# Gate and up products of four feed-forward layers as seven half-size products in Strassen's manner, with the sums of their operands made on the chip

## Chip, core and metric

The kernel runs as one program on one core of a Trainium2 chip. The metric is the device time of one execution in microseconds (us); lower is better. The engines are TensorE (PE: products, with its weight loads as PEld), VectorE (DVE), ScalarE (ACT), GpSimd (POOL) and SyncE (SP, which issues the DMAs here).

## What is computed

The network works on 512 tokens of 1024 features. A first block of two attention layers gives x; then come two layers, each of a feed-forward step, a mixer, a cross-attention and a second feed-forward step, and a last norm. The change is in the four feed-forward steps, of which the reference says:

```python
D_FF = ((8 * D_MODEL // 3 + 127) // 128) * 128      # 2816

def rmsnorm(x, g):
    xf = x.astype(jnp.float32)
    y = xf * lax.rsqrt(jnp.mean(xf * xf, axis=-1, keepdims=True) + NORM_EPS)
    return (y * g.astype(jnp.float32)).astype(x.dtype)

def swiglu(h, w_in, w_out):
    gate, up = jnp.split(h @ w_in, 2, axis=-1)
    return (jax.nn.silu(gate) * up) @ w_out
```

A step is x + 0.5 * swiglu(rmsnorm(x, g), w_in, w_out), with w_in of 1024 x 5632 and w_out of 2816 x 1024, everything in float32.

## The kernel before

Activations have their features on partitions: x is eight tiles `xr` of [128, 512 tokens]. A float32 operand a is kept as hi + lo (hi its rounding to float32r), and a product is three passes, hi\*hi, hi\*lo and lo\*hi: `Net.mm3` (L127) issues the three matmuls of a chunk of 128 features on L131, L132 and L133. `Net.split` (L113) makes hi by a copy on ACT (L114) and lo by a subtraction on DVE (L115), whose two inputs lie in SBUF. `Net.weight` (L117) loads a weight piece of 512 KB into `ws` (three buffers, in a pool that lives through the whole program) by a DMA that SP issues (L121), and splits it into `wh`, `wl` of [128, 1024] (four buffers each).

A feed-forward step, `Block2.ffn` (L1185), begins with `norm` (L1125): for each chunk of x, hi and lo of x times the norm's gain (`nh`, `nl`, L1132 on ACT and L1133 on DVE), and its square, summed over the chunks by POOL into `acc` (L1141). The tiles `nh`, `nl` and `acc` are in the pool `norm`, which is opened once for all steps. `stats` (L1144) makes `rb`, 1/rms of each token along rows, by two small products and a chain of small DVE instructions (`Net.rsqrt`, L145 to L155).

Then 22 chunks j of 128 hidden features follow in groups of 8, 8 and 6. For each j there is a gate product `pg` and an up product `pu`, each of 8 chunks of features x 3 passes, a matmul with 512 columns (tokens) each time. After them:

```python
t = pool.tile([P, S], F32, name="g", tag="g")
nc.vector.tensor_tensor(t, pg, self.rb, op=OP.mult)
nc.scalar.activation(t, t, AF.Silu)
nc.gpsimd.tensor_tensor(out=t, in0=t, in1=self.rb, op=OP.mult)
u = pool.tile([P, S], F32, name="u", tag="u")
nc.vector.tensor_tensor(u, pu, t, op=OP.mult)
```

and u is split into `hh`, `hl`. These are lines L1197 to L1204. When a group's hidden chunks are there, eight output products add to x (L1212); in the very last group they run in two cuts of 256 tokens, so that the last norm can follow the first cut.

No order is written out by hand in a feed-forward step: a scheduler, which goes by a timeline of its own, places each engine's instructions. Each engine then runs its instructions in that order and waits for semaphores. Pools of a stage are opened and closed with it, and a later pool that gets the same memory waits until the earlier one's last reader is done.

## Time and profile before

| | us |
|---|---|
| median of 3 runs (range) | 3713.2 (3712.51 to 3716.09) |
| span of the profiled execution | 3715.2 |
| PE busy | 3618.4 (97%) |
| PE weight loads busy | 2996.4 (81%) |
| DVE busy | 2070.7 (56%) |
| ACT busy | 1375.2 (37%) |
| POOL busy | 762.7 (21%) |

The span is that of one profiled execution; it is 2.0 us above the median of the timed runs. Busy shares are averages over the whole program. Matmuls overlap in the array, so a PE that is 97% busy says that products follow each other with hardly a pause; what one product costs is the distance between the starts of two that follow each other. An instruction's recorded time on DVE or POOL includes the time it is held up after it has started.

### The profile page before, as it was taken

The page shows a single profiled execution, that of the slowest core. Times are in us where ns is not written, and L with a number is a line of the kernel's source. Part 1 is how long each engine was busy: PE and PEld are TensorE (multiplying, and loading weights), DVE is VectorE, ACT ScalarE, POOL GpSimd, SP SyncE. Part 2 cuts the span into 40 slices and gives each one's busy share as a digit, 9 for nine tenths or more (in the row PEclk, how much of TensorE's full clock was granted, in tenths as well). Part 3 has the DMA queues.
Part 4 walks back from the last instruction along what each step waited for, and adds up shares of the span by engine and source line. Part 5 has one row for each costly group of instructions (what it writes and reads, how often), then busy time and mean ns, then how long its engine had stood idle before and what let it go on. Part 6 is the DMA issues. An engine that isn't in the chain of part 4 may idle for free.

```text
span 3715.2 us, 51467 instructions
## 1 busy us (share of the span) xinstructions
PE 3618.4 (97%) x19706; PEld 2996.4 (81%) x19706; DVE 2070.7 (56%) x4209; ACT 1375.2 (37%) x2407; POOL 762.7 (21%) x908
## 2 busy tenths in 40 slices
PE   8999999999999999999999999999999999999998
PEld 6887778888887778888778888888888888788887
DVE  6665763376566464334766433443347887664335
ACT  4334443233345432223654322322233333443223
POOL 1222330032233011102320100210025444101001
PEclk9999999999999999999999999999999999999999
DMA  8434113143322333333122333333333212322333
GB/s 276 128 111 136 58 49 128 63 142 88 88 70 67 139 100 102 97 94 105 58 91 63 108 97 97 97 97 97 97 100 112 57 56 74 115 75 93 101 98 103
DMA packets 135718, 364.35 MB, mean 98 GB/s; under 512 B 30000, under 2 KB 43184, under 8 KB 134960
## 3 DMA queue, kind: packets, MB, share of 16 engines
q1 hardware_dynamic: 135472, 361.06, 31.2%
q8 instruction: 155, 2.54, 0.3%
q14 instruction: 91, 0.75, 0.1%
HBM read 331.64 MB, written 19.66 MB: 95 GB/s over the span
## 4 chain that ended last, share of the span: by engine, by line
PE 87%; DVE 6%; ACT 2%; DMA 2%; issue 1%; POOL 1%; SPq 0%; DVEq 0%; ACTq 0%; POOLq 0%
PE p L131 15%; PE p L133 15%; PE p L132 15%; PE pS L131 7%; PE pS L132 6%; PE pS L133 6%; PE po L519 2%; PE pT L132 2%; PE pT L131 2%; PE pT L133 2%; PE po L132 2%; PE po L131 2%; PE po L133 2%; DVE wl L115 1%; PE pS L493 1%
## 5 line engine op out<-in xcount | busy, mean ns | idle before, releaser
L114 ACT ACTIVATE wh<-ws 128x1024 fp32r<-128x1024 f32 (+4 forms) x561 | 563.7, 1006 | 1421.8 <-PE p L132 683.8
L115 DVE TENSOR_TENSOR wl<-ws,wh 128x1024 fp32r<-128x1024 f32 (+3 forms) x542 | 640.4, 1182 | 252.7 <-ACT wh L114 250.8
L131 PE MATMUL p<-nh,wh 128*128 128x512 f32 x1084 | 429.1, 397 | 4.5 <-ACT nh L1132 2.0
L133 PE MATMUL p<-nh,wl 128*128 128x512 f32 x1084 | 424.7, 392 | 4.7 <-DVE wl L115 4.7
L132 PE MATMUL p<-nl,wh 128*128 128x512 f32 x1084 | 424.2, 391 | 1.9 <-DVE nl L115 1.9
L1199 POOL TENSOR_TENSOR g<-g,rb 128x512 f32<-128x512 f32 x88 | 149.8, 1704 | 1137.1 <-ACT g L1198 1137.1
L131 PE MATMUL pS<-nh,wh 128*128 128x512 f32 x620 | 254.5, 411 | 1.0 <-DVE xr L1182 1.0
L133 PEld LDWEIGHTS p<-nh,wl 128*128 128x128 f32 x1084 | 203.5, 188 | 50.3 <-DVE wl L115 6.2
L133 PE MATMUL pS<-nh,wl 128*128 128x512 f32 x620 | 242.8, 392 | 0.0
L132 PE MATMUL pS<-nl,wh 128*128 128x512 f32 x620 | 242.6, 391 | 0.0
L131 PEld LDWEIGHTS p<-nh,wh 128*128 128x128 f32 x1084 | 203.6, 188 | 46.8 <-ACT nh L1132 2.5
L132 PEld LDWEIGHTS p<-nl,wh 128*128 128x128 f32 x1084 | 203.7, 188 | 42.2 <-DVE nl L115 2.2
L1197 DVE TENSOR_TENSOR g<-p,rb 128x512 f32<-128x512 f32 x88 | 60.4, 691 | 227.8 <-PE p L133 217.6
L131 PE MATMUL p<-hxh,wh 128*128 128x512 f32 (+1 forms) x456 | 183.9, 403 | 0.8 <-DVE wT L502 0.8
L132 PE MATMUL p<-hl,wh 128*128 128x512 f32 (+1 forms) x488 | 179.8, 369 | 0.0
L133 PE MATMUL p<-hh,wl 128*128 128x512 f32 (+1 forms) x488 | 179.4, 368 | 0.0
L131 PE MATMUL p<-hh,wh 128*128 128x512 f32 (+1 forms) x488 | 179.3, 368 | 0.0
L1141 POOL TENSOR_TENSOR acc<-acc,sq 128x512 f32<-128x512 f32 x48 | 73.5, 1532 | 477.4 <-ACT sq L1140 477.0
L133 PE MATMUL p<-hxh,wl 128*128 128x512 f32 (+1 forms) x456 | 170.5, 374 | 0.0
L132 PE MATMUL p<-hxl,wh 128*128 128x512 f32 (+1 forms) x456 | 170.5, 374 | 0.0
L509 POOL TENSOR_SCALAR p<-p,rinv 128x768 f32<-128x768 f32 (+2 forms) x128 | 104.3, 815 | 254.0 <-DVE rinv L508 145.7
L1212 DVE SCALAR_TENSOR_TENSOR xr<-p,xr 128x512 f32<-128x512 f32 (+1 forms) x68 | 42.5, 627 | 170.0 <-PE p L133 169.9
(592 smaller groups left out, 8864.2 us busy)
## 6 DMA issues: line engine op xcount, KB each, us to landing
ws<-in_ffn_w_in_dram SPq DMA_DIRECT2D x176, 512.0 KB
ws<-in_ffn_w_out_dram SPq DMA_DIRECT2D x64, 512.0 KB
ws<-in_w_in_tok_dram SPq DMA_DIRECT2D x52, 512.0 KB
wh<-in_w_ada_dram SPq DMA_DIRECT2D x48, 512.0 KB
ws<-in_ffn_w_out_dram SPq DMA_DIRECT2D x40, 384.0 KB
ws<-in_w_out_dram SPq DMA_DIRECT2D x24, 512.0 KB
ws<-in_dn_qkv_dram SPq DMA_DIRECT2D x24, 512.0 KB
ws<-in_xa_wk_dram SPq DMA_DIRECT2D x16, 512.0 KB
```

The costliest lines, as they stand in the source:

```text
L114: self.last_hi = self.nc.scalar.activation(hi, src, AF.Copy)
L115: (eng or self.nc.vector).tensor_tensor(out=lo, in0=src, in1=hi.bitcast(F32), op=OP.subtract)
L131: mm(pt, sh, mh, start=first and i == 0, stop=False)
L132: mm(pt, sh, ml, start=False, stop=False)
L133: mm(pt, sl, mh, start=False, stop=last and i == n - 1)
L493: mm(ps, q, kA[:, k0:k1], start=True, stop=False)
L509: nc.gpsimd.tensor_scalar(p, p, r, 0.5, op0=OP.mult, op1=OP.mult)
L519: self.net.nc.tensor.matmul(ps[h:h + HD, :], v, w, start=i < 2, stop=i >= len(parts) - 2)
L1141: (nc.vector if c == 7 else nc.gpsimd).tensor_tensor(out=acc, in0=acc, in1=sq, op=OP.add)
L1197: nc.vector.tensor_tensor(t, pg, self.rb, op=OP.mult)
L1199: nc.gpsimd.tensor_tensor(out=t, in0=t, in1=self.rb, op=OP.mult)
L1212: nc.vector.scalar_tensor_tensor(x, ps, 0.5, x, op0=OP.mult, op1=OP.add)
```

## The change

The two products of a chunk j, gate and up, are taken as one product of [512 tokens x 1024] with [1024 x 256], each side cut in half: tokens and features of x into X11, X12, X21, X22, and the weight into B11, B21 (gate) and B12, B22 (up). `USES` names the seven products: P1 to P7, each over 512 features (4 chunks x 3 passes, matmuls with 256 columns), with operands that are blocks or sums of blocks. Outside the feed-forward steps the program's source is the same (comments and descriptions are gone, so lines after the first move by a few).

`halves` takes the place of `norm` in these steps: it scales each chunk of x into `xg`, forms S1 to S4 of the tokens' side, and splits the seven tokens' operands into hi and lo; `xg`, `xh` and the temporaries are in pools that are opened in the step. `sums` loads the weights of a chunk j into `wg`, `wu` (four buffers, in the step's own pool) and forms T3 and T1 on DVE, T2 and T4 on POOL. `operands` splits seven weight operands of [128, 512]. `gated` adds the products up: some are accumulated in a PSUM bank, with copies of the bank between (`s1`, `sV`, `sU`, on ACT), and the gate, in two halves of 256 tokens, goes through DVE, POOL, ACT and POOL again. PE's order is written out by hand in the loop over j; P3 and P4 of a chunk come after P1, P7 and P6 of the next. The other engines' order is still the scheduler's.

```diff
+    USES = dict(P1=("X11", "B11"), P2=("X12", "B21"), P3=("S4", "B22"), P4=("X22", "T4"), P5=("S1", "T1"),
+                P6=("S2", "T2"), P7=("S3", "T3"))
...
+        for c in range(8):
+            if c % 2 == 0:
+                xg.append(hold.tile([P, 2 * S], F32, name="xg", tag="hd", bufs=8))
+            v = xg[-1].rearrange("p (h c t) -> p h c t", h=2, c=2)[:, :, c % 2, :]
+            nc.scalar.activation(v, self.x[c].rearrange("p (h t) -> p h t", h=2), AF.Copy, scale=g[:, c:c + 1])
+            p = c // 2 % 2
+            if c % 2:
+                a11, a21 = xg[p][:, :S], xg[p][:, S:]
+                if c < 4:
+                    put("X11", p, a11)
+                    s3 = tmp("s3", "t")
+                    nc.vector.tensor_tensor(s3, a11, a21, op=OP.subtract)
+                    put("S3", p, s3)
+                else:
...
+    def sums(self, wg, wu, pool):
...
+        G, U = (pool.tile([P, 1024], F32, name=n, tag="wr", bufs=4) for n in ("wg", "wu"))
+        nc.sync.dma_start(G, wg)
+        nc.sync.dma_start(U, wu)
+        B = dict(B11=G[:, :512], B21=G[:, 512:], B12=U[:, :512], B22=U[:, 512:])
+        for n, a, b, eng in (("T3", "B12", "B22", nc.vector), ("T1", "B11", "B12", nc.vector),
+                             ("T2", "T1", "B22", nc.gpsimd), ("T4", "T2", "B21", nc.gpsimd)):
+            B[n] = pool.tile([P, 512], F32, name=n, tag=n, bufs=2)
+            eng.tensor_tensor(out=B[n], in0=B[a], in1=B[b], op=OP.add)
+        return B
...
+        def gate(sl, snap, bank):
+            v, rb = t[:, sl], self.rb[:, sl]
+            nc.vector.tensor_tensor(v, ps[bank], st[snap], op=OP.add)
+            nc.gpsimd.tensor_tensor(out=v, in0=v, in1=rb, op=OP.mult)
+            nc.scalar.activation(v, v, AF.Silu)
+            nc.gpsimd.tensor_tensor(out=v, in0=v, in1=rb, op=OP.mult)
...
-                for j in range(k0, k0 + kn):
-                    pg = self.fm(win[l, j], self.h)
-                    pu = self.fm(win[l, 22 + j], self.h)
...
+                        mm(j, made, "P1")
+                        mm(j, made, "P7")
+                        if more:
+                            operands(j + 1, "B11", "T3")
+                        if cur:
+                            mm(j - 1, cur, "P3")
+                        mm(j, made, "P6")
+                        if cur:
+                            mm(j - 1, cur, "P4")
+                        operands(j, "B22", "T4")
...
+                        mm(j, made, "P2")
+                        if more:
+                            operands(j + 1, "T2", "B21")
+                        if j:
+                            mm(j, made, "P5")
+                        if more:
+                            operands(j + 1, "T1")
```

The output products of a group (`ffn_out`) take the first two chunks of x without the group's last hidden chunk, and add that after; they are the same products as before.

How the order of the instructions moves is shown at two places. The first is DVE in the loop over j, in the middle of a group. Before, one chunk j (L115 is lo of a split):

```order
L1197 TENSOR_TENSOR g<-p_15105,rb 128x512
L115 TENSOR_TENSOR wl<-ws,wh 128x1024
L1201 TENSOR_TENSOR u<-pS,g 128x512
L115 TENSOR_TENSOR wl<-ws,wh 128x1024
L115 TENSOR_TENSOR hl<-u,hh 128x512
```

In the changed kernel, the first twelve of the fifteen rows of a chunk (L116 is lo of a split; `hd` is the hidden chunk; `pS`, `po` and `p3` are PSUM banks):

```order
L1263 TENSOR_TENSOR T3_15090<-wu_15087 128x512
L1263 TENSOR_TENSOR T1_15092<-wg_15086,wu_15087 128x512
L1308 TENSOR_TENSOR u1_15080<-pS_14955,sU_15078 128x256
L116 TENSOR_TENSOR hd_14815<-u_14814,hd_14815 128x512
L116 TENSOR_TENSOR wl_15131<-wg_15086,wh_15130 128x512
L116 TENSOR_TENSOR wl_15131<-T3_15090,wh_15130 128x512
L1315 TENSOR_TENSOR u_14958<-p3_14954,t_14957 128x256
L1299 TENSOR_TENSOR t_14957<-pS_14955,sV_15017 128x256
L116 TENSOR_TENSOR wl_15183<-wu_14943,wh_15182 128x512
L116 TENSOR_TENSOR wl_15183<-T4_14952,wh_15182 128x512
L1299 TENSOR_TENSOR t_15101<-po_15100,s1_15116 128x256
L116 TENSOR_TENSOR wl_15205<-T2_15094,wh_15204 128x512
```

Five rows become fifteen: after these twelve come two more splits of weights (B21 and T1) and one product of two SBUF tiles of 256 columns (`u`, L1312). POOL has one instruction of 512 columns for a chunk before; now it has these six:

```order
L1263 TENSOR_TENSOR T2_15094<-T1_15092,wu_15087 128x512
L1263 TENSOR_TENSOR T4_15096<-T2_15094,wg_15086 128x512
L1300 TENSOR_TENSOR t_14957<-t_14957,rb_14765 128x256
L1300 TENSOR_TENSOR t_15101<-t_15101,rb_14765 128x256
L1302 TENSOR_TENSOR t_14957<-t_14957,rb_14765 128x256
L1302 TENSOR_TENSOR t_15101<-t_15101,rb_14765 128x256
```

The second place is ACT at the start of a feed-forward step that follows a cross-attention, with what each row waits for in brackets (a semaphore's name begins with the engine that raises it). Before, the scaled chunks `nh` stand between the work of the stage that ends:

```order
L114 ACTIVATE wh_18920<-ws_18918 128x1024 [waits DMAHW1_49,PE_49]
L1132 ACTIVATE nh_18837<-xr0_13651,cols_88 128x512 [waits PE_49]
L1140 ACTIVATE sq_18881<-xr6_13657 128x512 [waits DVE_49,Pool_49]
L1132 ACTIVATE nh_18842<-xr1_13652,cols_88 128x512 [waits PE_49]
L1132 ACTIVATE nh_18849<-xr2_13653,cols_88 128x512 [waits PE_49]
L114 ACTIVATE wh_19040<-ws_19038 128x1024 [waits DMAHW3_49,PE_49]
L1132 ACTIVATE nh_18856<-xr3_13654,cols_88 128x512
```

In the changed kernel, where PE_49 of the first row of `xg` counts up to the last matmul of the stage before:

```order
L1249 ACTIVATE sq_21691<-xr6_13657 128x512 [waits DVE_49,Pool_49]
L1225 ACTIVATE xg_21618<-xr0_13651,cols_88 128x2x256 [waits PE_49]
L1225 ACTIVATE xg_21618<-xr1_13652,cols_88 128x2x256
L1225 ACTIVATE xg_21635<-xr2_13653,cols_88 128x2x256
L1225 ACTIVATE xg_21635<-xr3_13654,cols_88 128x2x256
L1225 ACTIVATE xg_21654<-xr4_13655,cols_88 128x2x256
L1225 ACTIVATE xg_21654<-xr5_13656,cols_88 128x2x256
L1225 ACTIVATE xg_21689<-xr6_13657,cols_88 128x2x256
L1225 ACTIVATE xg_21689<-xr7_13658,cols_88 128x2x256 [waits DVE_49]
L1249 ACTIVATE sq_21721<-xr7_13658 128x512 [waits Pool_49]
L115 ACTIVATE nh_21622<-xg_21618 128x512 [waits Activation_49]
```

All eight scalings now stand behind that last matmul, and behind them every split of the tokens' operands. On DVE the rows of this preparation stand behind the last addition to x; the product P6 of the first chunk needs the 33rd of them, here in its place:

```order
L1238 TENSOR_TENSOR s1_21699<-xg_21689,xg_21635 128x512
L1239 SCALAR_TENSOR_TENSOR s2_21700<-xg_21635,s1_21699 128x512
L116 TENSOR_TENSOR wl_21807<-wu_21606,wh_21806 128x512
L1242 SCALAR_TENSOR_TENSOR s4_21701<-s2_21700,xg_21689 128x512
L116 TENSOR_TENSOR wl_21807<-T4_21615,wh_21806 128x512
L116 TENSOR_TENSOR xh_21705<-s2_21700,xh_21704 128x512
```

The last of these rows is the one that P6 needs. It was no row of the kernel before, whose 16 instructions for `nh` and `nl` were all that a step's products waited for.

## Rows read from the trace of the kernel before

**Rows 1.** The page: span, and busy time of PE, with its share.

```profile
span 3715.2 us, 51467 instructions
...
PE 3618.4 (97%) x19706; PEld 2996.4 (81%) x19706; DVE 2070.7 (56%) x4209; ACT 1375.2 (37%) x2407; POOL 762.7 (21%) x908
```

**Rows 2.** Windows: four starts of a feed-forward step, then four chunks j.

```profile
core 0: us, PE busy (x) PEld busy (x) DVE busy (x) ACT busy (x) POOL busy (x), PEclk, DMA share, GB/s
...
1360.40:1390.00 29.60, 27.59 (x127) 22.26 (x126) 19.12 (x28) 14.73 (x22) 9.41 (x6) 1.00 0.23 72
2030.00:2060.00 30.00, 30.00 (x132) 24.29 (x130) 21.45 (x27) 16.93 (x26) 8.57 (x6) 1.00 0.46 142
2385.00:2415.00 30.00, 30.00 (x134) 24.86 (x133) 19.00 (x24) 16.95 (x24) 9.74 (x6) 1.00 0.39 119
3315.00:3345.00 30.00, 30.00 (x131) 24.26 (x130) 21.71 (x27) 17.07 (x25) 8.57 (x6) 1.00 0.48 149
...
1502.30:1545.83 43.53, 43.53 (x194) 36.05 (x193) 17.70 (x21) 12.82 (x16) 7.12 (x5) 1.00 0.30 97
```

**Rows 3.** Timeline of PE, 512 columns: start us, us, instruction; first and tenth.

```profile
2379.77 0.39 PE L131 MATMUL p<-hh,wh 128*128 128x512 f32 x1
...
2381.81 0.39 PE L131 MATMUL p<-hh,wh 128*128 128x512 f32 x1
```

**Rows 4.** Timeline of PE, 256 columns (last group): first and thirteenth.

```profile
3679.48 0.28 PE L133 MATMUL p<-hh,wl 128*128 128x256 f32 x1
...
3680.92 0.28 PE L133 MATMUL p<-hh,wl 128*128 128x256 f32 x1
```

**Rows 5.** Groups by shape: instruction, count | busy us, mean ns | idle before.

```profile
L133 PEld LDWEIGHTS p<-nh,wl 128*128 128x128 f32 x1076 | 202.7, 188 | 49.2 <-DVE wl L115 6.2
L115 DVE TENSOR_TENSOR hl<-u,hh 128x512 fp32r<-128x512 f32 x88 | 60.4, 689 | 0.0
L526 DVE TENSOR_TENSOR o<-po,vl 64x256 f32<-64x256 f32 x80 | 33.1, 414 | 26.5 <-ACT vl L525 25.6
L114 ACT ACTIVATE hh<-u 128x512 fp32r<-128x512 f32 x88 | 55.7, 634 | 3.8 <-DVE u L1201 2.7
L525 ACT ACTIVATE vl<-po 64x256 f32<-64x256 f32 x80 | 30.5, 381 | 57.8 <-PE po L519 48.5 <-issue 8.3
L1140 ACT ACTIVATE sq<-xr 128x512 f32<-128x512 f32 x56 | 34.5, 618 | 2.0 <-POOL acc L1141 1.1 <-DVE xr L1182 0.8
L154 DVE TENSOR_TENSOR rt<-rt,rv 128x4 f32<-128x4 f32 x120 | 22.2, 185 | 3.3
L1199 POOL TENSOR_TENSOR g<-g,rb 128x512 f32<-128x512 f32 x88 | 149.8, 1704 | 1137.1 <-ACT g L1198 1137.1
```

**Rows 6.** Timeline of DVE: two instructions that wait for nothing between them.

```profile
1389.66 1.29 DVE L1197 TENSOR_TENSOR g<-p,rb 128x512 f32<-128x512 f32 x2 [5.85 <-ACT rb L164]
```

**Rows 7.** Timeline of DVE and of POOL at 2942 us.

```profile
2942.51 1.23 DVE L115 TENSOR_TENSOR wl<-ws,wh 128x1024 fp32r<-128x1024 f32 x1 [0.17 <-ACT wh L114]
2943.65 1.77 DVE L1490 SCALAR_TENSOR_TENSOR z<-z,zh 128x512 f32<-128x512 f32 x1
...
2943.51 1.36 POOL L1646 TENSOR_TENSOR B<-U,lev 128x512 f32<-128x512 f32 x1 [4.46 <-PE pT L1650]
```

**Rows 8.** Timeline of DVE and of POOL at 1364 us (512 columns) and 3698 us (256).

```profile
1364.96 9.93 DVE L1133 SCALAR_TENSOR_TENSOR nl<-xr,cols,nh 128x512 fp32r<-128x512 f32 x7 [1.32 <-ACT nh L1132]
...
1363.88 9.80 POOL L1141 TENSOR_TENSOR acc<-acc,sq 128x512 f32<-128x512 f32 x6 [133.29 <-ACT sq L1140]
...
3698.00 2.19 DVE L1950 TENSOR_TENSOR y<-y,rb 128x256 f32<-128x256 f32 x3 [0.33 <-ACT rb L164]
...
3698.04 4.30 POOL L1950 TENSOR_TENSOR y<-y,rb 128x256 f32<-128x256 f32 x5 [34.55 <-ACT rb L164]
```

**Rows 9.** Timeline of POOL and of DVE at 1392 us; `po` is in PSUM.

```profile
1392.60 4.79 POOL L1199 TENSOR_TENSOR g<-g,rb 128x512 f32<-128x512 f32 x3 [18.92 <-ACT g L1198]
...
1393.93 0.69 DVE L1201 TENSOR_TENSOR u<-po,g 128x512 f32<-128x512 f32 x1 [1.23 <-POOL g L1199]
```

More of the change, by code (lines that the diff above doesn't have):

```diff
@@ L2 @@
 from contextlib import ExitStack
+from functools import partial
 from itertools import chain, islice
@@ L125, in weight, with mm3 @@
         return h.rearrange("p (k c) -> p k c", k=nk), l.rearrange("p (k c) -> p k c", k=nk)
-    def mm3(self, pt, items, first=True, last=True):
+    def mm3(self, pt, items, first=True, last=True, more=False):
         mm, n = self.nc.tensor.matmul, len(items)
+        if more:
+            mm = partial(mm, skip_group_check=True)
         for i, (sh, sl, mh, ml) in enumerate(items):
@@ new lines, in operands, with product @@
+    def operands(self, B, W, *names):
+        net = self.net
+        h = net.whi.tile([P, 1024], F32R, name="wh", tag="wh")
+        l = net.wlo.tile([P, 1024], F32R, name="wl", tag="wl")
+        for i, n in enumerate(names):
+            sl = slice(i * 512, (i + 1) * 512)
+            net.split(B[n], h[:, sl], l[:, sl])
+            W[n] = tuple(a[:, sl].rearrange("p (k c) -> p k c", k=4) for a in (h, l))
+    def product(self, n, W, ps, first=True):
+        x, b = self.USES[n]
+        wh, wl = W[b]
+        self.net.mm3(ps, [(wh[:, k, :], wl[:, k, :], *self.X[x][k]) for k in range(4)], first=first, more=not first)
@@ new lines, in gated, with copy, up, last @@
+    def gated(self, pool, hold, hid):
+        net, nc = self.net, self.net.nc
+        H = self.HT
+        ps = dict(a=net.psum("p3")[:, :H], d=net.psum("pS")[:, :H], e=net.psum("po")[:, :H])
+        small = lambda name: pool.tile([P, H], F32, name=name, tag=name, bufs=1)
+        t = pool.tile([P, S], F32, name="t", tag="t", bufs=2)
+        u = pool.tile([P, S], F32, name="u", tag="u", bufs=2)
+        hd = hold.tile([P, 2 * S], F32R, name="hd", tag="hd", bufs=8)
+        hid.append((hd[:, :S], hd[:, S:]))
+        st = {}
+        def copy(n):
+            st[n] = small(n)
+            nc.scalar.activation(st[n], ps["a"], AF.Copy)
+        def gate(sl, snap, bank):
[4 more added lines that the diff above has]
+            nc.gpsimd.tensor_tensor(out=v, in0=v, in1=rb, op=OP.mult)
+        lo, hi = slice(0, H), slice(H, S)
+        def up():
+            copy("sU")
+            st["u1"] = small("u1")
+            nc.vector.tensor_tensor(st["u1"], ps["d"], st["sU"], op=OP.add)
+        def last():
+            gate(hi, "sV", "d")
+            nc.vector.tensor_tensor(u[:, hi], st["u1"], t[:, hi], op=OP.mult)
+            net.split(u, hd[:, :S], hd[:, S:])
+        return ps, dict(P1=lambda: copy("s1"), P7=lambda: None, P6=lambda: copy("sV"), P2=lambda: gate(lo, "s1", "e"), P5=up,
+                        P3=lambda: nc.vector.tensor_tensor(u[:, lo], ps["a"], t[:, lo], op=OP.mult), P4=last)
@@ L1187, in ffn @@
+    def ffn(self, n, l, out=None):
         net, nc = self.net, self.net.nc
         win, wout = net.I[f"{n}_w_in"], net.I[f"{n}_w_out"]
[L1189 to L1206 removed]
@@ L1207, in ffn @@
                     part = [(hi[:, t0:t1], lo[:, t0:t1]) for hi, lo in hid]
                     for c in range(8):
[L1209 to L1210 removed]
+                        ps = self.fm(wout[l, c, :, k0 * P:(k0 + kn) * P], part, net.psum("ps")[:, :t1 - t0])
                         x = self.x[c][:, t0:t1]
[L1212 removed]
@@ L1213, in ffn, with ffn_out, part @@
-                    if after and k0 == 16:
-                        after(t0, t1)
+                        nc.vector.scalar_tensor_tensor(x, ps, -0.5, x, op0=OP.mult, op1=OP.add)
+                    final(t0, t1)
+    def ffn_out(self, wout, hid, k0, kn):
+        net, nc = self.net, self.net.nc
+        early = []
+        def part(c, ks):
+            if len(early) <= c:
+                early.append((net.psum(None), net.weight(wout[c, :, k0 * P:(k0 + kn) * P], kn)))
+            ps, (wh, wl) = early[c]
+            net.mm3(ps, [(wh[:, k, :], wl[:, k, :], *hid[k]) for k in ks], first=0 in ks, last=kn - 1 in ks)
+            if kn - 1 in ks:
+                nc.vector.scalar_tensor_tensor(self.x[c], ps, -0.5, self.x[c], op0=OP.mult, op1=OP.add)
+        for c in range(2):
+            part(c, range(kn - 1))
+        for c in range(2):
+            part(c, (kn - 1,))
+        for c in range(2, 8):
+            part(c, range(kn))
@@ L1978, in model @@
             b2.ffn("ffn2", l)
-    with tc.tile_pool(name="fin", bufs=1) as pool:
-        b2.ffn("ffn2", 1, ((0, 256), (256, 512)), b2.final(out, pool))
+    b2.ffn("ffn2", 1, out)
 def _constants():
```

99 lines of the change are left out of this document (81 added, 18 removed).

## The prediction

> **What bounds the kernel now.** I read the page first, for the shares, then windows over the feed-forward steps, then the timeline of PE there for the distance between products, and last the timelines of DVE and POOL for what they cost when both work. The page shows PE busy for 97% of 3715.2 us [rows 1]. The windows say that this holds where the change is made: four chunks j take 43.53 us, PE is busy in all of them, and DVE in 17.70 (41%), ACT in 12.82, POOL in 7.12 [rows 2]. Three of the four feed-forward steps begin with no pause of PE in the 30 us around the start; the first loses 2.0 us (29.60 less 27.59) [rows 2]. So the steps are bound by PE's products and nothing else, and fewer columns would be worth having, as long as the other engines keep up.
>
> **What PE saves.** Products of 512 columns start 2.04 us / 9 = 0.227 us apart [rows 3], products of 256 columns 1.44 us / 12 = 0.120 us apart [rows 4]: half the columns cost a little over half. A chunk j has 48 matmuls of 512 columns before, 48 x 0.227 = 10.88 us, which is a quarter of the 43.53 us. Now it has 7 x 4 x 3 = 84 of 256 columns, 84 x 0.120 = 10.08 us. That is 0.80 us for each of 88 chunks, **-70 us**, the most that the change can bring. The output products are the same.
>
> The weight loads double in share: one of 0.188 us [rows 5] for each 0.120 us product. The products of 256 columns in rows 4 have their own loads too, one each, and still start 0.120 us apart, so I cost the loads at nothing. The Trainium skill ("TensorE: Matmul & The Clock Gate", Part 3, The mechanism) says that a weight load overlaps with a product in flight only where the two use different row groups of the array, which tiles of 128 rows never do. The trace disagrees (0.120 us, loads included); by that rule a chunk would take its products and its loads one after the other, an estimated 84 x (0.120 + 0.188) = 25.9 us.
>
> **The loop over j, on DVE and POOL.** Here the order of DVE (the first place shown) grows from 5 rows to 15, and POOL's from 1 to 6. The price of a row depends on the other engine. At 2943 us POOL starts while DVE's `wl` runs, and ends 1.13 us after `wl` has ended; DVE's `z`, which started early in that, ends 0.55 us after POOL's end [rows 7]. Each waits for the other to finish: a DVE instruction with two SBUF inputs and a POOL instruction of 512 columns take 1.13 + 0.55 = 1.68 us as a pair. At 1364 us six POOL additions among seven such DVE instructions take 9.80 us, 1.63 us a pair; with 256 columns five take 4.30 us, 0.86 us a pair [rows 8], of which 0.28 is DVE's (half of 0.55) and 0.58 POOL's. A DVE instruction with an input in PSUM is not held up: `u` takes its usual 0.69 us while POOL works [rows 9].
>
> A chunk now has on DVE ten two-input SBUF instructions of 512 columns (seven splits of weights, T3, T1, the split of u), one of 256, and four of 256 columns from PSUM; all six of POOL's read SBUF. With DVE's queue never empty, two of the ten are paired with T2 and T4, 2 x 1.68 = 3.36 us; four with POOL's 256-column products, 4 x (0.55 + 0.58) = 4.52 us; four run alone, 0.60 us apart (1.29 - 0.69) [rows 6], 2.40 us; the short one takes 0.41 [rows 5] less 0.09 of overlap, about 0.33 us, as do the four from PSUM, of which one (`u1`, right behind T1, when T2 starts) lies beside POOL's work: 0.33 + 3 x 0.33 = 1.32 us. The sum is **11.6 us**, above the 10.08 of PE: DVE becomes the bound, and PE waits, at the latest where P5 needs the bank's copy `sV`, whose buffer DVE's gate addition of the chunk before has to free.
>
> The Trainium skill ("SBUF — State Buffer", SBUF: two separate sides) says that the engine that starts first holds the ports they share for its whole instruction. The rows agree on who waits, but a waiting instruction needs less than its usual time afterwards (0.55 us of 0.69); with whole instructions, a chunk would come to an estimated 12.8 us.
>
> Ends of this term: 10.6 us if all four PSUM instructions lie beside POOL's work; 12.5 us if none does and each of six handovers also loses the overlap of 0.09 us. I take 11.6, the pairing that the order shows. It does not hold for every chunk: a group's first chunk has its operands from the time of the output products before, and its last makes none for a next. I count the stretches between two gate additions that carry the whole set: 6 + 6 + 4 in a step, 64 in all. 64 x (11.6 - 10.08) = **+98 us** (ends 33 and 155). ACT's share, 8 x 0.634 + 3 x 0.381 and two short ones [rows 5], stays below 8 us a chunk.
>
> **The starts of the steps.** Before, `nh` and `nl` lie in a pool that is always open, and were made chunk by chunk while the stage before was still multiplying; hence no pause. Now `xg`, the temporaries and half of the operands lie in pools opened with the step, and the second place of the order shows the outcome: the first scaling waits for PE's last matmul, and all the preparation stands behind it. After a cross-attention: eight scalings on ACT at 0.62 us (as `sq` [rows 5]) are 5.0 us, the first rounding 0.63. From there DVE has 27 rows (7th to 33rd) until P6 of the first chunk can end, 27 x 0.60 = 16.2 us, and POOL's T2 and T4 of two chunks hold them up 4 x 1.13 = 4.5 us: 26.3 us, in which PE has P1, P7 and half of P6 to do, 3.6 us. Pause: 22.7 us. Then `rb`: five more rows (3.0 us), twelve small ones at 0.185 us [rows 5] (2.2) and two splits between (1.2), against 2.2 us of PE's work: 4.2 us more. Together 27 us. The first step's start has the six POOL additions of `acc` in it too (6 x 1.13 = 6.8 us): 34, less the 2.0 it loses now. `ffn1` of the second layer follows a feed-forward step, and the weights of its first chunks are ready; P6 needs the 24th row: 5.6 + 18 x 0.60 - 3.6 + 4.2 = 17 us. Sum 27 + 27 + 32 + 17 = **+103 us**. Ends: 65 if POOL holds nothing up and the `rb` chain is hidden; 125 if the first weights, whose loads are also issued only then, land after the scalings. At 1360 us the granted clock stayed at 1.00 after the pause [rows 2]; no row shows it after 20 us, so half clock for the 7.2 us of a first chunk, 4 x 7.2 = 29 us, is at the upper end alone.
>
> **Ends of groups.** P3 of the last chunk follows P5 in the same bank at once, and waits for the copy `sU`, 0.38 us [rows 5] and two handovers: 0.5 x 12 = **+6 us**. The hidden chunk that comes last is covered: the output products of the other seven, for two chunks of x, are 2 x 21 x 0.227 = 9.5 us.
>
> **Sum.** -70 + 98 + 103 + 6 = +137 us on 3715.2, so 3852; the profiled execution is 2 us above the median, so **3850 us**.
>
> **Rivals.**
> - *The products alone count (faster).* If the preparation of a step is hidden as before and POOL's work falls into gaps of DVE, -70 + 6 and up to 30 for the starts: about 3665 us. For it: DVE is 41% busy in the loop [rows 2]. Against it: the pairs of rows 7 and 8, and the wait on PE's last matmul. It decides for faster only where starts and loop together cost less than 64 us.
> - *Starts exposed, loop bound by PE.* The loop runs at 10.08 us because POOL's instructions meet DVE less than I count: -70 + 103 + 6 = +39, 3752 us. Against it: even with every PSUM instruction hidden the loop stands at 10.6.
> - *Loop bound by DVE, starts half hidden.* If the preparation overlaps better than row by row: -70 + 98 + 52 + 6 = +86, 3799 us.
> - *Weight loads bound the products.* 84 x 0.188 = 15.8 us a chunk, 4.9 x 88 = +432 us, with the starts some 4250 us. Rows 4 speak against it. The Trainium skill ("TensorE: Matmul & The Clock Gate", Part 3, The mechanism) would have it so.
>
> **How the numbers follow.** Forecast 0.67, the second rival 0.11, the third 0.14, faster 0.05, loads 0.01, else 0.02. The forecast's own range is 3790 to 3910: low and high ends of both large terms together are unlikely. The range, 3755 to 3920, takes in the third rival too, and half of the second; it leaves out the other half, the faster one, and the outer ends. About 0.2% (7 us) is what a measurement of this kernel can tell from no change: faster 0.05, within it 0.02, slower 0.93.
>
> **What would show it.** PE pauses of 15 to 35 us at four places, each ended by a split on DVE; in the loop a distance of 11 to 12 us between chunks, DVE nearly always busy with its two-input instructions at a mean well above 0.69 us, and PE's idle time ended by DVE or by ACT's copies behind it. I am wrong if PE is busy without pause at the starts, or if chunks follow each other every 10.1 us.

## The result, and the profile after

The changed kernel takes 3976.4 us (median of 4 runs, 3972.4 to 3979.5), the kernel before 3714.6 beside it (3712.5 to 3718.2): a ratio of 1.0704, with a 95% interval of 1.0689 to 1.0719. It is slower, as forecast, but by 262 us where 137 were forecast, and above the range.

The page of the changed kernel, to be read against [rows 1]:

```profile
span 3977.7 us, 60647 instructions
...
PE 3630.6 (91%) x22874; PEld 3141.0 (79%) x22874; DVE 2737.0 (69%) x5145; ACT 1674.9 (42%) x3255; POOL 1262.3 (32%) x1348
```

PE, 97% busy before, now stands still for some 347 us (3977.7 less 3630.6). Where it does is seen first in windows: the four starts of a step, four chunks of the loop, the end of a group, and the 10 us behind that. The columns are those of [rows 2], which answer to the first five.

```profile
1363.00:1410.00 47.00, 17.14 (x75) 14.74 (x74) 39.84 (x55) 24.68 (x45) 19.24 (x12) 0.62 0.23 76
2123.00:2164.00 41.00, 18.25 (x78) 15.80 (x77) 33.59 (x55) 20.80 (x39) 10.22 (x7) 0.61 0.28 90
2549.00:2580.00 31.00, 17.72 (x82) 15.89 (x81) 24.39 (x47) 18.52 (x34) 3.26 (x2) 0.67 0.10 29
3533.00:3574.00 41.00, 18.39 (x79) 15.95 (x78) 33.60 (x55) 20.76 (x38) 10.28 (x7) 0.61 0.27 90
1441.70:1489.50 47.80, 41.33 (x339) 40.51 (x337) 47.80 (x62) 24.98 (x51) 29.79 (x24) 1.00 0.30 89
1489.00:1505.00 16.00, 7.16 (x44) 6.56 (x43) 11.13 (x15) 4.55 (x9) 7.81 (x7) 0.86 0.44 131
1505.00:1515.00 10.00, 10.00 (x40) 8.10 (x40) 2.87 (x4) 1.88 (x3) 1.88 (x2) 0.88 0.18 52
```

In the loop it is DVE that is busy all the time (47.80 of 47.80 us, where it had 17.70 of 43.53 before), and PE that has gaps. At the starts PE works for 36 to 57% of the window, at a granted clock of 0.61 to 0.67. The end of a group loses 9 of 16 us, and the clock is still down behind it. The next rows say what each group of hidden chunks costs: the last addition to x ahead of a step, at the end of its first group and at the end of its second, in the kernel before and then in the changed one (the second feed-forward step of the first layer).

```profile
2052.81 0.68 DVE L1182 TENSOR_TENSOR xr<-p,xr 128x512 f32<-128x512 f32 x1
2184.14 0.69 DVE L1212 SCALAR_TENSOR_TENSOR xr<-pS,xr 128x512 f32<-128x512 f32 x1 [3.35 <-PE pS L133]
2314.70 0.69 DVE L1212 SCALAR_TENSOR_TENSOR xr<-pS,xr 128x512 f32<-128x512 f32 x1 [3.35 <-PE pS L133]
```

```profile
2124.17 0.69 DVE L1185 TENSOR_TENSOR xr<-p,xr 128x512 f32<-128x512 f32 x1 [2.11 <-PE p L136]
2303.87 0.69 DVE L1401 SCALAR_TENSOR_TENSOR xr<-pS,xr 128x512 f32<-128x512 f32 x1 [4.15 <-PE pS L136]
2448.41 0.69 DVE L1401 SCALAR_TENSOR_TENSOR xr<-pS,xr 128x512 f32<-128x512 f32 x1 [4.15 <-PE pS L136]
```

A second group went from 130.6 to 144.5 us, 14 us more. A first group went from 131.3 to 179.7: the same 14, and 34 more for the start. The other three starts, read in the same way (a step's first group against its second), come to 37, 20 and 34, **126 us** for the four. Eight groups of eight chunks at 14 us (15 in the third step) and four groups of six at some 4 us are **131 us**. The rest of the 262, some 6 us, lies outside the steps: 3 ahead of the first, 3 between the third and the fourth.

**The loop.** One chunk on DVE, from the timeline, with the first row of the next:

```profile
1441.69 0.68 DVE L116 TENSOR_TENSOR wl<-T,wh 128x512 fp32r<-128x512 f32 x1
1442.30 0.41 DVE L1315 TENSOR_TENSOR u<-p,t 128x256 f32<-128x256 f32 x1
1442.63 0.41 DVE L1299 TENSOR_TENSOR t<-pS,sV 128x256 f32<-128x256 f32 x1
1442.96 0.67 DVE L116 TENSOR_TENSOR wl<-wu,wh 128x512 fp32r<-128x512 f32 x1
1443.56 1.22 DVE L116 TENSOR_TENSOR wl<-T,wh 128x512 fp32r<-128x512 f32 x1
1444.71 0.41 DVE L1299 TENSOR_TENSOR t<-po,s 128x256 f32<-128x256 f32 x1
1445.04 0.68 DVE L116 TENSOR_TENSOR wl<-T,wh 128x512 fp32r<-128x512 f32 x1
1445.64 1.22 DVE L116 TENSOR_TENSOR wl<-wg,wh 128x512 fp32r<-128x512 f32 x1
1446.78 1.22 DVE L116 TENSOR_TENSOR wl<-T,wh 128x512 fp32r<-128x512 f32 x1
1447.93 0.96 DVE L1312 TENSOR_TENSOR u<-u,t 128x256 f32<-128x256 f32 x1
1448.81 0.68 DVE L1263 TENSOR_TENSOR T<-wu 128x512 f32<-128x512 f32 x1
1449.41 0.68 DVE L1263 TENSOR_TENSOR T<-wg,wu 128x512 f32<-128x512 f32 x1
1450.02 0.41 DVE L1308 TENSOR_TENSOR u<-pS,sU 128x256 f32<-128x256 f32 x1
1450.35 1.67 DVE L116 TENSOR_TENSOR hd<-u,hd 128x512 fp32r<-128x512 f32 x1
1451.94 1.78 DVE L116 TENSOR_TENSOR wl<-wg,wh 128x512 fp32r<-128x512 f32 x1
1453.64 0.68 DVE L116 TENSOR_TENSOR wl<-T,wh 128x512 fp32r<-128x512 f32 x1
```

The wait of PE before P5, with the copy ahead of it, in a later chunk of the same group:

```profile
1490.92 0.38 ACT L1295 ACTIVATE sV<-p 128x256 f32<-128x256 f32 x1 [1.56 <-DVE t L1299]
1491.36 0.39 PE L134 MATMUL p<-nh,wh 128*128 128x256 f32 x1 [1.60 <-ACT sV L1295]
```

No row has a bracket: DVE never waits for data, and the chunk is as long as its queue, 1453.64 less 1441.69 = 11.95 us. The same kind of instruction takes 0.68 us or 1.22 (and 0.41 or 0.96), and 1.67 or 1.78 where POOL has 512 columns in T2 and T4: six of the fifteen rows meet one of POOL's six. PE waits at the place that the prediction named, before P5, for the copy sV, which waits for DVE's gate addition. There are 59 such pauses in the trace. Here and below a sum of pauses is counted from start to start, less the 0.12 us of a product, which gives somewhat more than the brackets: 1.73 us each, 102 us in all.

**The ends of groups.** DVE and PE at the end of the first group, from the timeline:

```profile
1493.19 0.69 DVE L1263 TENSOR_TENSOR T<-wu 128x512 f32<-128x512 f32 x1 [2.36 <-DMA wu<-in_ffn_w_in_dram]
...
1494.40 1.22 DVE L116 TENSOR_TENSOR wl<-ws,wh 128x1024 fp32r<-128x1024 f32 x1
...
1495.87 1.96 DVE L116 TENSOR_TENSOR wl<-ws,wh 128x1024 fp32r<-128x1024 f32 x1
...
1498.45 1.47 DVE L1312 TENSOR_TENSOR u<-u,t 128x256 f32<-128x256 f32 x1 [0.62 <-POOL t L1302]
...
1499.84 1.74 DVE L116 TENSOR_TENSOR wl<-ws,wh 128x1024 fp32r<-128x1024 f32 x1
...
1501.51 0.41 DVE L1308 TENSOR_TENSOR u<-pS,sU 128x256 f32<-128x256 f32 x1
...
1501.97 0.58 PE L134 MATMUL pS<-xh,wh 128*128 128x256 f32 x1 [5.87 <-DVE u L1308]
```

P4 of the last chunk adds to the bank that `u1` (L1308) has to read first, and PE stands still for 5.87 us until it has. `u1` needs only P5 and a copy, which was done at 1494.4; but in DVE's order it stands behind the sums of the next group's first chunk, which wait 2.36 us for a load and end at 1494.5, and behind three splits of output weights and a product that waits for POOL, which fill the time until 1501.5. There are eight such pauses of 6 us, behind groups that another group follows; behind the last group of a step it is 1.3 us. All pauses before P4 make 52 us, those before P3 16 us. Behind the long ones the granted clock stands at 0.50 for a time (0.88 on average in the last window above): 37 us of products in all at the eight ends, which costs up to half of that, some 19 us.

**The starts.** ACT and PE at the start of the second step, from the timeline:

```profile
2124.17 5.01 ACT L1225 ACTIVATE xg<-xr,cols 128x512 f32<-128x512 f32 x8 [1.38 <-PE p L136]
...
2130.79 0.58 PE L134 MATMUL p<-nh,wh 128*128 128x256 f32 x1 [6.66 <-ACT wh L115]
...
2144.52 0.58 PE L135 MATMUL p<-nh,wh 128*128 128x256 f32 x1 [7.60 <-DVE nh L116]
...
2151.86 0.39 PE L135 MATMUL p<-xh,wh 128*128 128x256 f32 x1 [1.36 <-DVE xh L116]
...
2160.47 1.11 PE L166 MATMUL pT<-c_ident,ry 128*128 128x128 f32 x4 [3.37 <-DVE ry L158]
```

All eight scalings follow PE's last matmul, as the order had shown. PE waits first for ACT's roundings, then for DVE's splits again and again (the last one for P6 at 2151.86), and at the end for the chain of `rb`. The pauses of the four starts make 98 us, of which 2 were there before. The granted clock is 0.50 for 126 us at the four starts: 240 products of 256 columns follow each other there by some 0.21 us instead of 0.12, some 22 us more.

### The profile page after: what moved, and what is told of

It is laid out like the page before. It is cut to its first block, busy times and chain, and to the rows that moved or that the text cites. A ratio compares the mean times of both kernels' runs of the same rounds, so it can differ in the third digit from the quotient of the medians.

```text
span 3977.7 us, 60647 instructions
## 1 busy us (share of the span) xinstructions
PE 3630.6 (91%) x22874; PEld 3141.0 (79%) x22874; DVE 2737.0 (69%) x5145; ACT 1674.9 (42%) x3255; POOL 1262.3 (32%) x1348
## 4 chain that ended last, share of the span: by engine, by line
PE 64%; DVE 19%; issue 6%; DMA 4%; ACT 4%; POOL 3%; SPq 0%; DVEq 0%; ACTq 0%; POOLq 0%
PE p L134 11%; PE p L135 11%; PE p L136 11%; DVE wl L116 8%; PE pS L134 5%; PE pS L135 5%; PE pS L136 5%; PE po L522 2%; POOL t L1300 1%; DVE u L1312 1%; DMA wu<-in_ffn_w_in_dram 1%; ACT wh L115 1%; PE po L135 1%; PE po L134 1%; PE po L136 1%
## 5 line engine op out<-in xcount | busy, mean ns | idle before, releaser
L115 ACT ACTIVATE wh<-ws 128x1024 fp32r<-128x1024 f32 (+3 forms) x385 | 375.3, 979 | 646.8 <-PE p L135 206.2
L116 DVE TENSOR_TENSOR wl<-ws,wh 128x1024 fp32r<-128x1024 f32 (+4 forms) x366 | 438.2, 1201 | 204.0 <-ACT wh L115 202.6
L134 PE MATMUL p<-nh,wh 128*128 128x256 f32 (+2 forms) x1260 | 421.5, 335 | 140.6 <-ACT sV L1295 92.6
L136 PE MATMUL p<-nh,wl 128*128 128x256 f32 (+2 forms) x1260 | 405.1, 322 | 7.6 <-DVE wl L116 7.6
L1300 POOL TENSOR_TENSOR t<-t,rb 128x256 f32<-128x256 f32 x176 | 183.5, 1043 | 688.0 <-DVE t L1299 682.0
L134 PEld LDWEIGHTS p<-nh,wh 128*128 128x128 f32 (+1 forms) x1260 | 245.6, 195 | 175.2 <-ACT sV L1295 107.3
L116 DVE TENSOR_TENSOR wl<-T,wh 128x512 fp32r<-128x512 f32 x352 | 316.7, 900 | 1.6 <-ACT wh L115 0.5
L135 PE MATMUL p<-nh,wh 128*128 128x256 f32 x880 | 255.2, 290 | 32.3 <-DVE nh L116 32.3
L115 ACT ACTIVATE wh<-T 128x512 fp32r<-128x512 f32 x352 | 218.8, 622 | 129.4 <-PE p L135 77.0
L136 PEld LDWEIGHTS p<-nh,wl 128*128 128x128 f32 (+1 forms) x1260 | 245.0, 194 | 26.5 <-DVE wl L116 9.8
L116 DVE TENSOR_TENSOR wl<-wg,wh 128x512 fp32r<-128x512 f32 x176 | 227.5, 1292 | 11.2 <-ACT wh L115 11.2
L1302 POOL TENSOR_TENSOR t<-t,rb 128x256 f32<-128x256 f32 x176 | 205.4, 1182 | 17.7 <-ACT t L1301 17.7
L134 PE MATMUL p<-hd,wh 128*128 128x512 f32 (+1 forms) x424 | 158.5, 375 | 0.6 <-ACT wh L115 0.6
L135 PE MATMUL p<-hd,wh 128*128 128x512 f32 (+1 forms) x424 | 157.3, 371 | 0.0
```

The costliest lines, as they stand in the source:

```text
L115: self.last_hi = self.nc.scalar.activation(hi, src, AF.Copy)
L116: (eng or self.nc.vector).tensor_tensor(out=lo, in0=src, in1=hi.bitcast(F32), op=OP.subtract)
L134: mm(pt, sh, mh, start=first and i == 0, stop=False)
L135: mm(pt, sh, ml, start=False, stop=False)
L136: mm(pt, sl, mh, start=False, stop=last and i == n - 1)
L1300: nc.gpsimd.tensor_tensor(out=v, in0=v, in1=rb, op=OP.mult)
```

## The experiments

Each kernel is the changed kernel with the edit shown, unless it says otherwise. Chunk distances are those between two instructions `u1`, one a chunk. Experiments 1 to 9 and 11 have one timed run each, and timed runs of one kernel lie up to 14 us apart (3682 to 3696 us in experiment 12); differences of that size are read from the lengths of groups in the traces instead.

**1. The second product by rb taken out of the loop.**

```diff
             nc.scalar.activation(v, v, AF.Silu)
-            nc.gpsimd.tensor_tensor(out=v, in0=v, in1=rb, op=OP.mult)
...
+                nc.vector.tensor_tensor(o, ps, self.rb, op=OP.mult)
```

> The second product of the gate by rb (two POOL instructions of 256 columns a chunk) is taken out of the loop; each output product is multiplied by rb once instead, on DVE out of PSUM. Theory A (DVE and POOL hold each other up on the memory side they share, so the loop runs at the length of DVE's queue with its pairs): two pairs of 1.13 us become two single instructions of 0.60 us, 1.06 us less of 11.95 us a chunk, 10.9 us; over some 60 chunks 64 us less than the changed kernel's 3977, about 3915 us. Theory B (the chain of waits around the buffer sV, P4 to gate addition to copy to P5, has its own length): the pause of 1.77 us before P5 stays, 11.95 us a chunk, 3977 us. Theory C (DVE's own fifteen rows fill the chunk, POOL or not): 11.95 us a chunk, 3977 us.

```profile
1580.26 0.41 DVE L1307 TENSOR_TENSOR u<-pS,sU 128x256 f32<-128x256 f32 x1
1591.23 0.41 DVE L1307 TENSOR_TENSOR u<-pS,sU 128x256 f32<-128x256 f32 x1
```

10.97 us a chunk and 3905.6 us: theory A, within 0.1 us a chunk. Two POOL instructions fewer shorten DVE's queue though DVE has not a row less in the loop. Of the 71 us, 55 are pauses before P5 and 19 pauses before P4, which theory A had not counted; a wait of 8 us for `acc` in the second mixer's norm is new (it is there in experiments 5 and 7 too, whose output products also go through a tile of the norm's pool).

**2. T2 and T4 on DVE.**

```diff
-                             ("T2", "T1", "B22", nc.gpsimd), ("T4", "T2", "B21", nc.gpsimd)):
+                             ("T2", "T1", "B22", nc.vector), ("T4", "T2", "B21", nc.vector)):
```

> T2 and T4 are formed on DVE instead of POOL: two rows more on DVE, two fewer on POOL. Theory A (pairs): 2 x 1.68 us of pairs become 4 x 0.60 us of single DVE instructions, 0.96 us less: 11.0 us a chunk, about 3920 us. Theory C (DVE's own rows fill the chunk): two rows of 0.60 us more, 13.1 us a chunk, about 4050 us. Theory B (chain around sV): 11.95 us or little more, about 3980 us.

```profile
1574.14 0.41 DVE L1308 TENSOR_TENSOR u<-pS,sU 128x256 f32<-128x256 f32 x1
1584.87 0.41 DVE L1308 TENSOR_TENSOR u<-pS,sU 128x256 f32<-128x256 f32 x1
```

10.73 us a chunk, 3863.9 us. DVE does two rows more and is done 1.2 us sooner, which ends theory C. The gain is larger than expected; 23 of the 113 us are at the ends of groups, where POOL's T2 and T4 had stretched the splits ahead of `u1`.

**3. Two buffers for sV.**

```diff
+        self.turn = not getattr(self, "turn", False)
+        small = lambda name: self.np_.tile([P, S], F32, name="acc", tag="acc", bufs=1)[:, :H] if name == "sV" and self.turn else pool.tile([P, H], F32, name=name, tag=name, bufs=1)
```

> The copy sV has two buffers in turn, so that the copy of a chunk need not wait for the gate addition of the chunk before; the work is the same. Theory B (chain around sV): the pause before P5 goes, 10.2 us a chunk, about 3870 us. Theories A and C (DVE's queue is the bound): PE waits elsewhere for the same time, 11.8 to 12 us a chunk, 3965 to 3985 us.

The trace of PE has the pause in another place, before P4 instead of P5:

```profile
1591.12 0.39 PE L134 MATMUL pS<-xh,wh 128*128 128x256 f32 x1 [1.60 <-DVE u L1309]
```

The chunks stay 11.95 us apart, and the time is 3957.8 us. Of what is saved, 7 us lie in the four first groups, 6 in the groups of six, 2 in the four second groups and 3 ahead of the first step. The wait only moved, to the next thing that DVE delivers late: theory B falls.

**4. u1 ahead of the next group's sums and the output weights.**

```diff
-                        if j + 1 < 22:
+                        if more:
                             raw[j + 1] = self.sums(win[l, j + 1], win[l, 23 + j], pool)
...
+                        with net.tc.issue_after(self.u1.ins):
+                            raw[j + 1] = self.sums(win[l, j + 1], win[l, 23 + j], pool)
...
+                with net.tc.issue_after(self.u1.ins):
+                    early.append((net.psum(None), net.weight(wout[c, :, k0 * P:(k0 + kn) * P], kn)))
```

> At a group's end the sums of the next group's first chunk and the splits of the output weights are queued on DVE behind u1, for which P4 of the last chunk waits; the loop is the same. Theory (order on DVE at a group's end): eight pauses of 6.1 us before P4 shrink to under 1 us, and the half clock behind each (6.8 us, worth 3.4) goes with them: 8 x 8.5 = 68 us less, about 3910 us. Rival (the weights themselves come late, by their load): P4 starts at once, but the output products behind it wait for their split weights as long as P4 did, 3965 to 3985 us.

3910.9 us, as the theory has it. The eight pauses before P4 are gone from the trace; the second group of the step shown takes 138.6 us where it took 144.5, and half clock is left behind two of the eight ends, for 3.4 us each, where it stood for 6.8 behind every one. By the traces the groups are 59 us shorter; 8 us more lie ahead of the first step, where the source is the same. Smaller pauses (18 us in all) stand among the output products now.

**5. Nothing on POOL in the loop** (edits 1 and 2, and the first product by rb on DVE too).

```diff
-            nc.gpsimd.tensor_tensor(out=v, in0=v, in1=rb, op=OP.mult)
+            nc.vector.tensor_tensor(out=v, in0=v, in1=rb, op=OP.mult)
```

> POOL has nothing left in the loop: T2 and T4 and the first product of the gate by rb are on DVE, the second product by rb is one for each output product. Theory A (pairs): DVE has 12 x 0.60 + 7 x 0.33 = 9.5 us of single rows a chunk, less than PE's 10.08, so PE bounds the loop: 10.1 to 10.3 us a chunk, pauses before P5 gone; 60 x 1.75 = 105 us, with some 23 us at the ends of groups and 18 us at the starts, where T2 and T4 no longer hold DVE up: about 3830 us. Rival (the order of the rows on DVE makes PE wait, pairs or not): a pause of 0.6 us or more stays, 10.7 us a chunk or more, 3870 us or more.

3839.1 us, theory A within 10 us. Of the pauses before P5 six short ones are left (2.9 us in all); the second group of the step shown takes 129.8 us, with 3.7 us of pauses left at its end, where the kernel before took 130.6. With POOL out of the way DVE carries the whole loop and PE is the bound again.

**6. Two whole chunks at the start of each step**, from `nh` and `nl` of the pool that is always open. The hidden chunks of the seven products carry a minus sign, which the output products take out again; this kernel leaves out that sign for the two whole chunks, so it does the same work for another result. Experiment 9 has the sign ("turned" in its expectation).

```diff
+                        ps = [self.fm(win[l, 0], self.h, net.psum("ps")), self.fm(win[l, 22], self.h, net.psum("ps"))]
+                        raw[n0] = self.sums(win[l, n0], win[l, 22 + n0], pool)
+                        next(stats)
+                        ps.append(self.fm(win[l, 1], self.h, net.psum("ps")))
+                        next(stats)
+                        ps.append(self.fm(win[l, 23], self.h, net.psum("ps")))
+                        tokens()
```

> The first two chunks of each step are whole products as in the kernel before, from tiles of the pool that is always open; the sums of the tokens' side are made beside them, and the blocks X11, X12 and X22 are halves of those tiles. The loop and the ends of groups are as in the changed kernel. Theory (the starts cost 96 us of pauses because all preparation waits for PE's last matmul, and 28 us of half clock behind them): both go; two chunks a step without the saving cost 8 x 0.80 = 6 us, and have no pause of 1.8 us, 14 us: 3977 - 124 + 6 - 14 = about 3845 us, granted clock 1.00 at the starts. Rival (DVE can't make the sums within two chunks): a pause of 10 us or more before the third chunk, 3890 us or more.

3890.6 us: the rival's number, though not in its place. The first step still paused for 22 us in all at its start, 6 for ACT's `nh` and most of the rest for `nl`, which DVE had behind its T sums; the second waited 3.6 us for `nh` and `nl` and 5.5 for `rb`. The four first groups are 80 us shorter than in the changed kernel, where the theory had 132.

**7. Experiments 4, 5 and 6 together**, and P3 and P4 of a group's last chunk behind a piece of the first output product; the sign is left out as in 6.

```diff
+        part(0, range(kn - 2))
+        tail()
+        for c in range(1, 3):
+            part(c, range(kn - 2))
```

> All together: two plain chunks at the start of a step, nothing on POOL in the loop, u1 ahead of the output weights, and P3 and P4 of a group's last chunk behind a piece of the first output product. If the four terms (loop 102 us, starts 96, ends of groups 68, half clock about 55) are separate, as the theory has it, what is left is the saving of PE, 80 x 0.80 = 64 us, less small pauses: 3650 to 3680 us. Rival (the terms are one shortage of DVE that only moves): pauses of 1 us or more a chunk come back in the loop, 3720 us or more.

3798.1 us: neither. The loop has no pauses to speak of (1.4 us in all), so the terms did not move into it, as the rival had it. But my own order made new ones: with P3 behind an output product, the split of that product's weight had to come ahead of `u1`, and stood behind it (4.2 us at each of eight ends). The starts were as in 6, but for the third, which waits 9 us where it waited 1.7.

**8. Unread products in the pauses of the starts.**

```diff
+            def warm(k):
+                for _ in range(k):
+                    nc.tensor.matmul(fill, net.ident, self.x[0], start=True, stop=True)
...
+                            warm(8)
```

> The changed kernel, with 8 products of 512 columns that nobody reads ahead of the first P1 of each step and 8 more in the middle of it, where PE would wait 7 and 8 us. Theory (PE's own pause makes the granted clock fall to half, which costs 28 us at the four starts): the pauses as such stay, the half clock goes in part or whole: 3950 to 3960 us. Rival (the clock falls for another reason, such as the rate of weight loads): half clock as before, 3977 us, or more by what the added products cost.

Windows around the same start, each from 4.2 us ahead of its first scaling, in the changed kernel and then with the unread products; the third column from the end is the granted clock:

```profile
2120.00:2165.00 45.00, 22.25 (x95) 19.24 (x94) 35.08 (x58) 22.41 (x41) 11.85 (x9) 0.63 0.25 82
```

```profile
2114.94:2159.94 45.00, 34.03 (x138) 23.24 (x137) 35.68 (x58) 23.27 (x41) 13.36 (x9) 0.89 0.24 82
```

The clock rose from 0.63 to 0.89, so it follows PE's pauses here, but the time fell by 7 us alone, to 3969.0, where the theory had 17 to 27. That is no more than two runs of one kernel can differ by. In the traces the four first groups are 4 us shorter in all, and the second groups 2 us longer. Of the 240 slowed products at the starts 138 are slow still, and some of the others stand ahead of a wait for DVE, which ends when DVE is done, at whatever clock PE runs.

**9. The starts of 6 with the order mended**, the operands of the whole chunks ahead of everything else.

```diff
-                        raw[n0] = self.sums(win[l, n0], win[l, 22 + n0], pool)
...
+                        with net.tc.issue_after(self.last_nh.ins), net.tc.issue_after(self.last_nl.ins):
+                            tokens()
+                            raw[n0] = self.sums(win[l, n0], win[l, 22 + n0], pool)
```

> As the kernel with two plain chunks, but ACT scales xg and DVE forms T and S sums only behind the last of the plain chunks' operands nh and nl, and the up product's sign is turned. There the starts still paused 19 us in the first step and 7 to 11 in the others, on nl behind T sums in DVE's order. Theory (the order of the rows on DVE and ACT at the start, not their amount, makes the pauses): under 5 us a start, 3891 less some 25: 3860 to 3870 us. Rival (DVE has too many rows in the first two chunks, in whatever order): the pauses move to the third chunk and to rb, 3880 to 3895 us.

3880.9 us, the rival's number, and the pauses moved to `rb`, as it said. Of the waits for `nh` and `nl` some 4 us are left, all in the first step; but the products for `rb` now wait at all four starts, 6.3 to 9.0 us by the brackets, 31 in all, where in experiment 6 they waited at two, for 8.5. Whether that is DVE's amount of work, with T2, T4 and the additions of `acc` on POOL beside it, or once more a place in an order, this run does not part. Experiment 10 puts these products one product (5.4 us) later and has nothing of the loop on POOL, and waits 2.6 to 3.4 us; with unread work on POOL the same order waits 6.6 to 7.7 (experiment 11).

**10. All together with the order mended** (7 and 9; the next sums behind the last split, the first output weight ahead of `u1`, and the banks multiplied by rb in place).

```diff
+                with net.tc.issue_after(self.u1.ins) if c else ExitStack():
+                    early.append((net.psum(None), net.weight(wout[c, :, k0 * P:(k0 + kn) * P], kn)))
...
+                            behind = net.last_lo
+                            with net.tc.issue_after(behind.ins):
+                                raw[j + 1] = self.sums(win[l, j + 1], win[l, 23 + j], pool)
```

> All edits together, with the order of DVE mended at starts and ends of groups: the sums of the next group's first chunk behind the last split of this group's hidden chunk, the first output weights ahead of u1, the chain of rb later, and no tile of the norm's used by the output products. Theory (loop, starts and ends are separate waits, each of which can be taken away): what stays is PE's saving of 80 x 0.80 = 64 us less 10 to 25 us of small pauses: 3660 to 3690 us, under the kernel before. Rival (DVE is short of time over the whole step, so pauses only move): 3730 us or more.

3696.4 us against 3714.3, a ratio of 0.9956 (0.9939 to 0.9973): faster than the kernel before, and 6 us above the theory's range. Windows over a start and over four chunks:

```profile
2051.00:2092.00 41.00, 38.12 (x235) 33.80 (x233) 36.49 (x74) 26.05 (x48) 0.56 (x1) 1.00 0.31 115
...
1505.00:1550.00 45.00, 44.97 (x368) 44.16 (x367) 40.36 (x80) 26.27 (x56) 0.00 (x0) 1.00 0.35 106
```

At this start, the second step's, PE loses 2.9 us, at full clock; in the loop it is never idle, and DVE is, for a tenth of the time.

**11. The same with work on POOL that nobody waits for.** This parts the two ways in which POOL could have cost time, by the shared memory side or by its results.

```diff
+        for i in range(4):
+            sl = slice(i * 256, (i + 1) * 256)
+            nc.gpsimd.tensor_tensor(out=junk[:, :256], in0=G[:, sl], in1=U[:, sl], op=OP.add)
```

> The kernel of all edits together (3696 us, a chunk every 10.2 us, nothing on POOL in the loop), with four POOL additions of 256 columns for each chunk, of two weight tiles in SBUF, whose result nobody reads: no instruction of the loop waits for them. Theory A (DVE and POOL hold each other up on the memory side they share): each meets a DVE instruction and adds 0.53 us to DVE, 9.5 + 2.1 = 11.6 us a chunk, over 60 chunks about 80 us: 3770 to 3800 us, and DVE's splits in the loop at a mean above 0.75 us. Rival (POOL's work in the changed kernel cost time only through the waits on its results): 10.2 us a chunk and 3690 to 3705 us as without it.

Groups by shape of experiment 10, then of this one:

```profile
L116 DVE TENSOR_TENSOR wl<-wg,wh 128x512 fp32r<-128x512 f32 x160 | 109.5, 684 | 0.9 <-ACT wh L115 0.6
```

```profile
L1258 POOL TENSOR_TENSOR acc<-wg,wu 128x256 f32<-128x256 f32 x320 | 376.1, 1175 | 892.7 <-DMA wu<-in_ffn_w_in_dram 822.2 <-PE po L1152 27.8 <-issue 13.7
L116 DVE TENSOR_TENSOR wl<-wg,wh 128x512 fp32r<-128x512 f32 x160 | 136.0, 850 | 0.3 <-ACT wh L115 0.3
```

3766.2 us, 70 more, for results that nobody reads; the splits go from 684 to 850 ns, and 50 us of pauses before P5 are back. It is theory A, with a smaller price: DVE is busy for 2730.8 us instead of 2606.2, 0.39 us for each of 320 additions, where 0.53 was expected.

**12. The products for rb behind P7 of the third chunk.**

```diff
                         mm(j, made, "P7")
+                        if j == n0:
+                            next(stats)
```

> The kernel of all edits together, with the two products that spread 1/rms of the tokens put behind P1 and P7 of the third chunk instead of ahead of them, where PE waited 3.0 us for the chain of small DVE instructions. Theory (that wait is a matter of the place in PE's order): 4 x 3 = 12 us less, 3680 to 3688 us. Rival (the gates of the plain chunks come later too and hold the banks that the next chunk needs): 3692 to 3700 us.

3686.1 us against 3712.8, a ratio of 0.9929 (0.9916 to 0.9941), as the theory has it. It is the fastest of these kernels. In the traces its groups take 24 us less than those of the kernel before, and another 7 us of the difference lie ahead of the first step, where the source is the same. Of the 40 us that are missing to PE's 64, 13 are lost in the first step's first group, 10 in the other three first groups, and 17 in the groups behind them.

## Why the prediction was right in direction and too small

- *The products* (-70 us): right. The loop's window has 339 products in 41.33 us of PE's time, 0.122 us each with their loads, so the rival of the weight loads falls.
- *The loop* (+98): right in cause, and in size partly by luck. Forecast were 11.6 us a chunk in 64 stretches, and 11.95 came, with 59 pauses of 1.73 us where 64 of 1.52 were forecast: two misses that nearly cancel. The listing shows the difference: the fourth of POOL's short products fell on the short `u` (0.96 us) and not on a split, and none of the four instructions that read PSUM lay beside POOL's work in a way that saved anything. Experiments 1 and 2 showed the price of a pair, 3 that the buffer is only where the wait shows, 11 that POOL's work costs DVE time even where nobody reads its results. The price of a pair with 256 columns, forecast as 1.13 us, came as 1.15. The Trainium skill ("SBUF — State Buffer", SBUF: two separate sides) says that the engine that starts first holds the ports that DVE and POOL share for its whole instruction. By that rule the prediction estimated 12.8 us, and 11.95 was measured, nearer to the prices of [rows 7, 8].
- *The starts* (+103): right in place and cause, too small by 23 us. The row count gave 26.3 us until P6 of the first chunk could end after a cross-attention, and the trace has 27.7 (2151.86 less 2124.17); the pauses of the four starts together grew by 96 us. What failed is "the granted clock stayed at 1.00", by which half clock stood at the upper end alone: the clock fell to 0.50 in all four starts, and slower products make some 22 us, 14 of them behind P6, where only the wait for `rb` can still hide a part. How much of that a full clock would give back stays open: experiment 8 brought back 4 us, with the clock restored in part.
- *The ends of groups* (+6): this is the step that failed. "The hidden chunk that comes last is covered" looked at the output products, which are indeed covered, and not at P4, which comes ahead of them and waits for `u1` in the bank. The order of DVE at the middle of a group was read row by row, that of its end was not. It cost 52 us before P4 and 16 before P3, and up to 19 us of half clock behind, 87 where 6 were forecast. Experiment 4 gave most of them back by order alone, 59 us in the groups.
- *The sum.* 81 us at the ends of groups, 23 at the starts and 4 in the loop make 108 of the 125 us missing. Some 6 us lie outside the steps, and 11 are not assigned. The range, to 3920, allowed for more at the starts and in the loop, but had no term for a wait at the end of a group.
- *The rivals.* That the products alone count was wrong for this kernel, but experiment 12 comes near it (3686 against some 3665 us), once each wait is taken away for itself. A loop bound by PE falls with the 11.95 us a chunk, and half hidden starts with their 126 us.

## What to carry to other kernels

A change that trades PE's columns for work on other engines has to be counted on the queue of the engine that gets the work, row by row, with the price of a row where the neighbour is busy; an engine at 41% on average had no room. Read the new order at every seam (start, middle and end of a loop), and for each product ask what is ahead of its releaser in that engine's queue. What POOL does for free may cost DVE more than doing it there.

## What was not expected of the hardware

- While POOL works on 512 columns, even DVE's instructions of 128x4 in the chain of `rb` take 1.13 us instead of 0.16 or 0.17 (two of them at 2155 and 2156 us in the changed kernel). The first of them ends as POOL does:

```profile
2155.25 1.13 DVE L152 TENSOR_SCALAR ry<-rb 128x4 int32<-128x4 int32 x1
...
2155.08 1.28 POOL L1263 TENSOR_TENSOR T<-T,wu 128x512 f32<-128x512 f32 x1 [15.98 <-DVE rv L148]
```

- In the loop, pauses of 1.4 to 1.6 us, one in every 12 us, left the granted clock at 1.00; the only longer one, of 1.90 us at 2343.6, was followed by half clock for 3.4 us, the eight of 5.7 to 6.1 us by half clock for 6.8 us, and the starts by more. Length alone does not decide: in experiment 4 pauses of 1.76 us at the ends of groups were followed by half clock at two of eight.
- With four POOL additions in a chunk, 0.39 us of DVE's time went to each, against the 0.55 by which a pair lengthened a row of 512 columns in the changed kernel's loop (1.15 us to the next row instead of 0.60): probably some of them met instructions that were not held up; no run counts them.
